# Query norms as the exponentials' scale, and per-head scaling on ScalarE, in a two-layer hybrid encoder trunk

## The chip, the cores and the metric

The kernel runs on one core of one Trainium2 chip. A core has TensorE (PE in the profile, with its weight loads shown as PEld), VectorE (DVE), ScalarE (ACT), GpSimd (POOL) and SyncE (SP), which here only issues DMAs. The time is the device time of one execution in microseconds. Before the change the median of three runs is 590.78 us (590.67 to 590.83).

## The reference

Two layers (`L = 2`) over 256 tokens of width 1024. Each layer normalizes `x`, makes one wide projection, feeds three token mixers (A: gated linear attention, B: sparse attention with an indexer that keeps 64 keys, C: differential attention), gates them, and adds the merged result to `x`:

```
h = _rms(x, norm_g[l]);  proj = h @ w_in[l]           # split into gq gk gv ga gz bq bk bv iq ik iw bz cq ck cv cz gate
_dsa:  q = _rms(bq, qn_g)   # 4 heads of 128;  k = _rms(bk, kn_g)
       p = softmax(q . k over the kept keys);  out = p @ bv
_diff: q = _rms(cq, qn_g)   # 4 heads x 2 halves of 64;  k = _rms(ck, kn_g)
       p = softmax(q_c . k_c) for c in (0, 1);  out = _rms((p0 - lam * p1) @ cv) * (1 - lambda_init)
x = x + (gated sum of y_a @ w_br0, y_b @ w_br1, y_c @ w_br2) @ w_out[l]
```

The part that the change concerns is `_rms` of the queries and keys: each row of each head is divided by its root mean square, which is one number per token and head, called the inverse norm `r` below. A row's softmax takes the maximum of its logits off before the exponential, and divides by the sum after it.

## The kernel before

**Matmuls.** All large products are in float32 precision built of three passes: an operand is held as a rounded high part and a low remainder, and `mm3` (L119) issues high by high, high by low and low by high. The weights stream in as *units* of 128 x 1024 float32. For each unit SyncE issues a DMA into `raw`, ScalarE copies it into `whi` (L234), VectorE subtracts to get `wlo` (L240), and TensorE does, for most projections, 12 matmuls of 128 x 512 with it. Five pairs of `whi`/`wlo` exist, so ScalarE can only begin a unit when TensorE has let go of the pair used five units earlier. Some units are sums of two weight matrices, made by GpSimd's accumulating DMAs (L208). Transposes go through TensorE too (L122).

**Order.** A table `ORDER` says which projection follows which (`bq, cq, ck, gate4, cz, bk, cv, gq, iq, ...`). The mixers are generators ("tasks") that are advanced between matmul groups by `Flow.pump`, and which yield a number of groups to wait. On top of this the framework schedules the program by its own timeline of the engines, so that the final order of the instructions on each engine can differ from the order in which they are written, and moves when an operation goes to another engine.

**Norms.** `headnorm` squares the whole 128 x 512 projection on ScalarE (L396, out of PSUM, the matmul's accumulators), sums the squares by head on VectorE (L398), has GpSimd make `r` (`rstd`: a multiply-add at L294, a power of -1/2 at L295), and multiplies the projection by `r` on VectorE into `qn` (L401). `qn` is transposed on TensorE (L122), and its high and low part are made by ScalarE (L414, L561) and VectorE. This is done for `bq`, `bk` (4 heads of 128) and for `cq`, `ck` (8 halves of 64), two token blocks each. Tiles of the tag `ev` (`sq`, `qn`, `th`) share two buffers; projections share four PSUM tiles (`pj`), logits and transposes four others (`at`).

**Softmaxes.** In `dsa_attend` the logits `blog` are masked on VectorE, the negated row maximum `negm` is taken on VectorE (L721), ScalarE makes the exponential with `negm` as its bias and the row sum as a second output (L688), VectorE multiplies the probabilities by the inverse sum (L730), and TensorE transposes them. In `diff_task` it is the same with L791 and L688; there the two softmaxes are joined on VectorE (L804) and transposed as `pT` (L122), which the products `av` take. Per layer there are three such logit tiles in the sparse attention and six in the differential one.

## Time and profile before

| | us |
|---|---|
| median of three runs | 590.78 (590.67 to 590.83) |
| profiled execution, first to last instruction | 589.0 |
| TensorE busy | 581.9 (99%) |
| VectorE busy | 494.4 (84%) |
| ScalarE busy | 382.9 (65%) |
| GpSimd busy | 89.7 (15%) |

The span of the profiled execution is the time between its first and last instruction; the page gives no other time of that execution. The 1.8 us between this span and the median lie outside the instructions. The granted TensorE clock is 1.000 over the whole span. A row of a group reads: line, engine, operation, output<-inputs, shape, count | busy us, mean ns of one | idle us just before and what ended it. A row of a timeline begins with its start and its length in us.

### The profile page before, as it was taken

What the parts mean: (1) busy time and instruction counts of PE and PEld (TensorE: products, weight loads), DVE (VectorE), ACT (ScalarE), POOL (GpSimd) and SP (SyncE); (2) the same over time, 40 slices, a digit from 0 to 9 for tenths busy, and PEclk for the clock granted to TensorE, in tenths of its full rate; (3) what the DMA queues carried; (4) which work ended last, traced back from release to release, by engine and by line L of the source; (5) the groups of instructions that cost most, each with busy time, mean ns of one, the idle gap of its engine ahead of it and who ended that gap; (6) DMA issues with size and microseconds to landing.
All of it is one profiled execution on the core that took longest, in us unless ns stands there. A gap on an engine that the chain in (4) does not pass through costs nothing.

```text
span 589.0 us, 8836 instructions
## 1 busy us (share of the span) xinstructions
PE 581.9 (99%) x3116; PEld 495.2 (84%) x3116; DVE 494.4 (84%) x815; ACT 382.9 (65%) x655; POOL 89.7 (15%) x121
## 2 busy tenths in 40 slices
PE   8999999999999999999999999999999999999997
PEld 4888888998888988888878888889888889888886
DVE  6878969988999899898687796797989998889962
ACT  6759668786658478464466775776866576656530
POOL 2032212002213031000020340300211221200000
PEclk9999999999999999999999999999999999999999
DMA  8654669428999679565446446862599994974821
GB/s 334 235 197 144 209 235 270 142 104 227 289 293 220 228 225 284 175 221 197 143 145 207 151 149 208 263 205 105 184 260 279 297 242 149 284 236 132 258 75 71
DMA packets 34027, 121.82 MB, mean 207 GB/s; under 512 B 3776, under 2 KB 4160, under 8 KB 33984
## 3 DMA queue, kind: packets, MB, share of 16 engines
q1 hardware_dynamic: 29376, 104.49, 50.5%
q0 software_dynamic: 4608, 16.78, 15.9%
q8 instruction: 24, 0.39, 0.3%
q14 instruction: 19, 0.16, 0.1%
HBM read 120.21 MB, written 1.05 MB: 206 GB/s over the span
## 4 chain that ended last, share of the span: by engine, by line
PE 96%; DVE 1%; DMA 1%; ACT 1%; issue 0%; POOL 0%; SPq 0%; DVEq 0%; POOLq 0%
PE q L119 13%; PE p L119 11%; PE gate L119 7%; PE out L119 7%; PE bz L119 4%; PE iq L119 4%; PE gq L119 4%; PE ck L119 4%; PE cq L119 4%; PE gz L119 4%; PE cz L119 4%; PE gv L119 4%; PE bv L119 4%; PE bk L119 4%; PE cv L119 4%; PE bq L119 3%
## 5 line engine op out<-in xcount | busy, mean ns | idle before, releaser
L234 ACT ACTIVATE whi<-raw 128x1024 fp32r<-128x1024 f32 x172 | 180.9, 1062 | 102.2 <-PE p L119 21.0
L240 DVE TENSOR_TENSOR wlo<-raw,whi 128x1024 fp32r<-128x1024 f32 x172 | 207.9, 1219 | 38.9 <-ACT whi L234 37.6
L234 ACT ACTIVATE whi<-sum 128x1024 fp32r<-128x1024 f32 x32 | 34.1, 1065 | 24.1 <-PE gz L119 5.4
L240 DVE TENSOR_TENSOR wlo<-sum,whi 128x1024 fp32r<-128x1024 f32 x32 | 39.5, 1235 | 4.2 <-ACT whi L234 3.7
L208 POOL DMA_DIRECT2D sum<-in_units x32 | 28.3, 883 | 84.0 <-DMA sum<-in_units 28.2
L294 POOL TENSOR_SCALAR v<-ss 128x4 f32<-128x4 f32 (+1 forms) x24 | 6.9, 288 | 224.0 <-DVE ss L398 91.5
L295 POOL TENSOR_TENSOR r<-v,half 128x4 f32<-128x4 f32 (+1 forms) x24 | 35.5, 1477 | 2.0
L119 PE MATMUL out<-wlo,mTh 128*128 128x512 f32 (+1 forms) x72 | 26.2, 368 | 0.0
L119 PE MATMUL out<-whi,mTh 128*128 128x512 f32 (+1 forms) x72 | 26.0, 366 | 0.0
L119 PE MATMUL out<-whi,mTl 128*128 128x512 f32 (+1 forms) x72 | 25.7, 368 | 0.0
L119 PE MATMUL q<-whi,sl 128*128 128x512 f32 x64 | 25.2, 394 | 0.0
L119 PE MATMUL q<-wlo,sh 128*128 128x512 f32 x64 | 25.1, 392 | 0.0
L119 PE MATMUL q<-whi,sh 128*128 128x512 f32 x64 | 24.9, 390 | 0.0
L119 PE MATMUL gate<-wlo,hTh 128*128 128x512 f32 x64 | 24.9, 390 | 0.0
L119 PE MATMUL p<-wlo,yTh 128*128 128x512 f32 x64 | 24.9, 389 | 0.0
L119 PE MATMUL gate<-whi,hTl 128*128 128x512 f32 x64 | 24.8, 390 | 0.0
L119 PE MATMUL p<-whi,yTl 128*128 128x512 f32 x64 | 24.6, 389 | 0.0
L119 PE MATMUL gate<-whi,hTh 128*128 128x512 f32 x64 | 24.5, 393 | 0.0
L119 PE MATMUL p<-whi,yTh 128*128 128x512 f32 x64 | 24.1, 392 | 0.0
L119 PE MATMUL q<-whi,hTh 128*128 128x512 f32 x48 | 19.2, 400 | 0.0
L119 PE MATMUL q<-whi,hTl 128*128 128x512 f32 x48 | 18.8, 391 | 0.0
L119 PE MATMUL q<-wlo,hTh 128*128 128x512 f32 x48 | 18.8, 391 | 0.0
(352 smaller groups left out, 1748.8 us busy)
## 6 DMA issues: line engine op xcount, KB each, us to landing
raw<-in_units SPq DMA_DIRECT2D x176, 512.0 KB, 4.5
sum<-in_units POOLq DMA_DIRECT2D x32, 512.0 KB, 7.9
sum<-in_units SPq DMA_DIRECT2D x16, 512.0 KB, 6.1
wsr<-in_wsmall SPq DMA_DIRECT2D x2, 416.0 KB, 7.0
xe<-in_x SPq DMA_DIRECT2D x1, 584.0 KB, 3.4
x<-in_x SPq DMA_DIRECT2D x1, 512.0 KB, 7.9
out<-xe SPq DMA_DIRECT2D x2, 256.0 KB, 2.0
pt<-in_ptmp SPq DMA_DIRECT2D x1, 384.0 KB, 9.5
```

The costliest lines, as they stand in the source:

```text
L119: return self.put(nc.tensor.matmul(*a, **k))
L208: G.dma_start(self.sums[l, "t3" if what == "t3" else "t1", pair, i], units[u + i], accum_op=OP.add)
L234: a = A.activation(hi, raw, AF.Copy)
L240: self.splits[j] = (a, V.tensor_sub(lo, raw, hi.bitcast(F32)))
L294: G.tensor_scalar(v, ss, 1.0 / dim, EPS, op0=OP.mult, op1=OP.add)
L295: G.tensor_tensor(r, v, half[:, :n], op=OP.pow)
```

## The change

The projection's squares of `bq` and `bk` (4 heads) are made by four ScalarE instructions per tile, one for each head, with the sum as a second output: VectorE's sum goes. For `cq` and `ck` (8 halves) square and sum stay as they were. The queries `bq` and `cq` are no longer multiplied by `r`: `qn` is a plain copy on ScalarE that needs no `r`. GpSimd copies `r` into a tile `rq`, and the softmaxes use it as the exponential's scale; so the row maximum, taken by VectorE into a tile `max`, has to be multiplied by `r` as well, which a new GpSimd instruction does (`scaled_max`) before the exponential can use it as bias. For the differential attention `rc` is a copy of `rq` in the order of its logits. The sparse keys `bk` are multiplied by `r` on ScalarE, four instructions per tile (`ck` stays on VectorE). The sparse probabilities are multiplied by their inverse sum on ScalarE instead of VectorE, one instruction per head as before. No matmul and no weight DMA is added or removed.

```diff
+    def squares(ps, nh, dh):
+        ss = tiny(nh, "ss")
+        if nh == 4:
+            junk = ev([P, CH], BF16, "sq")
+            for h in range(nh):
+                hs = slice(h * dh, h * dh + dh)
+                A.activation(junk[:, hs], ps[:, hs], AF.Square, accum_out=ss[:, h:h + 1])
+        else:
+            sq = ev([P, CH], F32, "sq")
+            A.activation(sq, ps, AF.Square)
+            V.tensor_reduce(ss, sq.rearrange("p (h d) -> p h d", h=nh), axis=AX, op=OP.add)
+        return rstd(ss, nh, dh)
+
+    def plain(ps):
+        n = ev([P, CH], F32, "qn")
+        A.activation(n, ps, AF.Copy)
+        return n
+
     def headnorm(ps, nh, dh):
-        sq = ev([P, CH], F32, "sq")
-        A.activation(sq, ps, AF.Square)
-        ss = tiny(nh, "ss")
-        V.tensor_reduce(ss, sq.rearrange("p (h d) -> p h d", h=nh), axis=AX, op=OP.add)
-        r = rstd(ss, nh, dh)
+        r = squares(ps, nh, dh)
         n = ev([P, CH], F32, "qn")
-        V.tensor_tensor(n.rearrange("p (h d) -> p h d", h=nh), ps.rearrange("p (h d) -> p h d", h=nh),
-                        r.unsqueeze(2).to_broadcast([P, nh, dh]), op=OP.mult)
+        if nh == 4:
+            for h in range(nh):
+                hs = slice(h * dh, h * dh + dh)
+                A.activation(n[:, hs], ps[:, hs], AF.Copy, scale=r[:, h:h + 1])
+        else:
+            V.tensor_tensor(...)
         return n
...
+        rq = {}
+
+        def row_scale(mark, nh, ps):
+            r = rq[mark] = sp.tile([P, nh], F32, tag="rq", bufs=8, name=nm("rq"))
+            G.tensor_copy(r, squares(ps, nh, CH // nh))
+            return plain(ps)
+
         def cq_task(mark, ps, dst):
-            n = headnorm(ps, 8, 64)
+            n = row_scale(mark, 8, ps)
...
         def qk_task(mark, ps, nh, dh, gain, hi, lo):
-            n = headnorm(ps, nh, dh)
+            n = row_scale(mark, nh, ps) if mark[:2] == "bq" else headnorm(ps, nh, dh)
...
-        def softmax_rows(ps, j, S, p, negm, sums, i):
-            A.activation(p, ps[:, j], AF.Exp, bias=negm[:, i:i + 1], accum_out=sums[:, i:i + 1])
+        def softmax_rows(ps, j, S, p, negm, sums, i, r):
+            A.activation(p, ps[:, j], AF.Exp, bias=negm[:, i:i + 1], scale=r[:, i:i + 1], accum_out=sums[:, i:i + 1])
+
+        def scaled_max(negm, r, ps, i):
+            m = tiny(ps.shape[1], "max")
+            V.tensor_reduce(m, ps, axis=AX, op=OP.max, negate=True)
+            G.tensor_tensor(negm[:, i], m, r[:, i], op=OP.mult)
...
-                V.tensor_reduce(negm[:, h0:h0 + per], ps, axis=AX, op=OP.max, negate=True)
+                scaled_max(negm, rq[f"bq{t}"], ps, slice(h0, h0 + per))
...
-                V.tensor_scalar_mul(p, p, rs[:, h:h + 1])
+                A.activation(p, p, AF.Copy, scale=rs[:, h:h + 1])
...
+            rc = sp.tile([P, 8], F32, tag="rc", bufs=2, name=nm("rc"))
+            G.tensor_copy(rc.rearrange("p (c h) -> p c h", c=2), rq[f"cq{t}"].rearrange("p (h c) -> p c h", c=2))
...
-                    V.tensor_reduce(negm[:, i0:i0 + per], ps, axis=AX, op=OP.max, negate=True)
+                    scaled_max(negm, rc, ps, slice(i0, i0 + per))
```

The framework's schedule puts the instructions in another order. Three places matter below. In the rows a name's number is that of its tile; the second program counts its tiles otherwise, so numbers differ between the two.

ScalarE at the start of the second layer, before the change: after the last square of `x` comes the square of `bq` for the first tokens, and then the eight evacuations of `h`, transposed, of the second tokens (`hps` into `hTh`), for which TensorE waits there.

```order
L320 ACTIVATE junk_3353,ss_77<-x 128x512
L396 ACTIVATE sq_3568<-bq_3417 128x512
L341 ACTIVATE hTh<-hps_3359,xe 128x128
L341 ACTIVATE hTh<-hps_3360,xe 128x128
L341 ACTIVATE hTh<-hps_3367,xe 128x128
```

The same place after the change:

```order
L320 ACTIVATE junk_3397,ss_77<-x 128x512
L400 ACTIVATE sq_3614,ss_3613<-bq_3461 128x128 x4
L409 ACTIVATE qn_3624<-bq_3461 128x512
L341 ACTIVATE hTh<-hps_3403,xe 128x128
L341 ACTIVATE hTh<-hps_3404,xe 128x128
```

Four squares and the copy of `bq` now stand where one square stood, ahead of the evacuations.

TensorE in the projection `iq` of the first layer, where the differential attention's probabilities of the first tokens (`cp`) are transposed into `pT`, before the change (`whi_786` is the third of the four weight units of `iq`):

```order
L119 MATMUL iq_1381<-hTh,whi_786 128x256
L119 MATMUL iq_1381<-hTl,whi_786 128x256
L119 MATMUL iq_1381<-hTh,wlo_787 128x256
L122 MATMUL pT_1366<-xe,cp_1219 128x128 x4
L119 MATMUL iq_1381<-hTh,whi_786 128x256
```

And after it (`whi_759` is the second unit, `whi_798` the third; this is the second of the four passes that `iq` makes over its units, where the rows above are of the first):

```order
L119 MATMUL iq_1419<-hTh,whi_759 128x256
L122 MATMUL pT_1404<-xe,cp_1245 128x128
L119 MATMUL iq_1419<-hTl,whi_759 128x256
L119 MATMUL iq_1419<-hTh,wlo_760 128x256
L122 MATMUL pT_1404<-xe,cp_1245 128x128
L119 MATMUL iq_1419<-hTh,whi_798 128x256
L122 MATMUL pT_1404<-xe,cp_1245 128x128
```

The transposes come 22 instructions later in the program, at 542 instead of 520, and one by one among matmuls of the projection.

TensorE in the projection `gv` of the first layer, before the change (the first and the second half of the tokens are `gv_1692` and `gv_1693`; `whi_905`, `whi_951` and `whi_979` are the second, third and fourth unit):

```order
L119 MATMUL gv_1692<-whi_905,hTl 128x512
L119 MATMUL gv_1692<-whi_951,hTh 128x512
L119 MATMUL gv_1693<-whi_887,hTh 128x512
...
L119 MATMUL gv_1693<-whi_951,hTl 128x512
L119 MATMUL gv_1692<-whi_979,hTh 128x512
L119 MATMUL gv_1692<-wlo_980,hTh 128x512
```

And after it (`whi_917`, `whi_963` and `whi_991` are the second to the fourth unit):

```order
L119 MATMUL gv_1730<-whi_917,hTl 128x512
L119 MATMUL gv_1730<-whi_963,hTh 128x512
...
L119 MATMUL gv_1730<-whi_963,hTl 128x512
L119 MATMUL gv_1730<-whi_991,hTh 128x512
L119 MATMUL gv_1730<-wlo_992,hTh 128x512
```

The first tokens now take all four units one after the other before the second tokens begin, so the fourth unit is used after 18 matmuls of `gv` and not after 36.

More of the change, by code (lines that the diff above doesn't have):

```diff
@@ L392, in proj_first @@
         yield p1
-    def headnorm(ps, nh, dh):
-        sq = ev([P, CH], F32, "sq")
-        A.activation(sq, ps, AF.Square)
-        ss = tiny(nh, "ss")
-        V.tensor_reduce(ss, sq.rearrange("p (h d) -> p h d", h=nh), axis=AX, op=OP.add)
-        r = rstd(ss, nh, dh)
-        n = ev([P, CH], F32, "qn")
-        V.tensor_tensor(n.rearrange("p (h d) -> p h d", h=nh), ps.rearrange("p (h d) -> p h d", h=nh),
-                        r.unsqueeze(2).to_broadcast([P, nh, dh]), op=OP.mult)
+    def squares(ps, nh, dh):
[14 more added lines that the diff above has]
+        return n
+    def headnorm(ps, nh, dh):
+        r = squares(ps, nh, dh)
+        n = ev([P, CH], F32, "qn")
+        if nh == 4:
[3 more added lines that the diff above has]
+        else:
+            V.tensor_tensor(n.rearrange("p (h d) -> p h d", h=nh), ps.rearrange("p (h d) -> p h d", h=nh),
+                            r.unsqueeze(2).to_broadcast([P, nh, dh]), op=OP.mult)
         return n
@@ L720, in dsa_attend @@
                                        op0=OP.mult, op1=OP.add)
-                V.tensor_reduce(negm[:, h0:h0 + per], ps, axis=AX, op=OP.max, negate=True)
+                scaled_max(negm, rq[f"bq{t}"], ps, slice(h0, h0 + per))
                 prob[h0] = w2([P, per, S], F32, "bp")
                 for j in range(per):
-                    softmax_rows(ps, j, S, prob[h0][:, j], negm, sums, h0 + j)
+                    softmax_rows(ps, j, S, prob[h0][:, j], negm, sums, h0 + j, rq[f"bq{t}"])
                 yield 1
@@ L790, in diff_task @@
                     V.memset(ps[0:64, :, S - 64:], NEG)
-                    V.tensor_reduce(negm[:, i0:i0 + per], ps, axis=AX, op=OP.max, negate=True)
+                    scaled_max(negm, rc, ps, slice(i0, i0 + per))
                     p = w2([P, per, S], F32, "cp")
                     for j in range(per):
-                        softmax_rows(ps, j, S, p[:, j], negm, sums, i0 + j)
+                        softmax_rows(ps, j, S, p[:, j], negm, sums, i0 + j, rc)
                     prob[h0, c] = p
```

## The prediction

> **What bounds the kernel now.** I read the head of the page first, then the stretches of the span in the table of windows (columns: stretch, its length, busy us and instructions of PE, PEld, DVE, ACT, POOL, then granted clock, DMA share, GB/s), then the groups.
>
> ```profile
> span 589.0 us, 8836 instructions
> PE 581.9 (99%) x3116; PEld 495.2 (84%) x3116; DVE 494.4 (84%) x815; ACT 382.9 (65%) x655; POOL 89.7 (15%) x121
> PE 96%; DVE 1%; DMA 1%; ACT 1%; issue 0%; POOL 0%; SPq 0%; DVEq 0%; POOLq 0%
> ```
>
> ```profile
> 14.30:296.30 282.00, 281.98 (x1513) 241.87 (x1513) 244.29 (x402) 187.31 (x317) 43.69 (x58) 1.00 0.69 212
> 296.30:299.00 2.70, 2.03 (x12) 1.14 (x11) 1.73 (x4) 2.65 (x8) 0.02 (x1) 1.00 0.74 223
> 299.00:587.00 288.00, 286.54 (x1556) 246.61 (x1554) 239.49 (x388) 183.06 (x309) 42.03 (x53) 1.00 0.64 197
> ```
>
> TensorE is busy without a hole in both layers, and the chain of waits is 96% TensorE. Being busy isn't yet being at its pace, so I looked at the pace in the chain:
>
> ```profile
> 209.01 10.91 PE gate L119 x48
> 198.46 6.99 PE bz L119 x58
> ```
>
> 48 matmuls of 512 columns take 10.91 us, 227 ns each, and 58 of (nearly all) 256 columns 6.99 us, 120 ns each; stretches of the same shapes go at the same pace whatever runs beside them. TensorE sets the time, the others follow. At the layer boundary 2.70 − 2.03 = 0.67 us are open; the first 14.3 us end before any instruction that the change touches. So an engine that gets faster has almost nothing to give, and the change can lose time wherever it makes TensorE wait. The cover against that is the stock of weights:
>
> ```profile
> L234 ACT ACTIVATE whi<-raw 128x1024 fp32r<-128x1024 f32 x172 | 180.9, 1062 | 102.2 <-PE p L119 21.0
> L240 DVE TENSOR_TENSOR wlo<-raw,whi 128x1024 fp32r<-128x1024 f32 x172 | 207.9, 1219 | 38.9 <-ACT whi L234 37.6
> ```
>
> ScalarE idled 102.2 us ahead of its weight copies, mostly because TensorE had not yet released a buffer, and VectorE 38.9 us behind ScalarE. With all pairs full, four units of 12 x 0.227 = 2.72 us lie ahead of TensorE: 10.9 us.
>
> **What is removed from VectorE.**
>
> ```profile
> L398 DVE TENSOR_REDUCE ss<-sq 128x4 f32<-128x512 f32 x8 | 5.4, 678 | 0.7 <-ACT sq L396 0.7
> L401 DVE TENSOR_TENSOR qn<-cq,r 128x512 f32<-128x512 f32 x4 | 2.8, 690 | 5.1 <-POOL r L295 5.1
> L401 DVE TENSOR_TENSOR qn<-bq,r 128x512 f32<-128x512 f32 x4 | 2.8, 690 | 1.2 <-POOL r L295 1.2
> L401 DVE TENSOR_TENSOR qn<-bk,r 128x512 f32<-128x512 f32 x4 | 2.7, 682 | 0.6 <-POOL r L295 0.6
> L730 DVE TENSOR_SCALAR bp<-bp,rs 128x256 f32<-128x256 f32 x8 | 3.0, 440 | 0.0
> L730 DVE TENSOR_SCALAR bp<-bp,rs 128x128 f32<-128x128 f32 x8 | 1.7, 272 | 0.0
> ```
>
> These six rows go entirely: 5.4 + 2.8 + 2.8 + 2.7 + 3.0 + 1.7 = 18.4 us, and VectorE falls from 494 to 476 us. None of it was on TensorE's path, so it is worth 0.
>
> **What is added to ScalarE.**
>
> ```profile
> L396 ACT ACTIVATE sq<-bq 128x512 f32<-128x512 f32 x4 | 2.4, 591 | 1.8 <-PE bq L119 1.8
> L916 ACT ACTIVATE junk<-go 128x128 f32<-128x128 f32 x16 | 4.2, 282 | 0.0
> L916 ACT ACTIVATION_READ_ACCUMULATOR junk<-go 128x1 f32 x16 | 3.4, 215 | 0.0
> 199.32 0.26 ACT L916 ACTIVATE junk<-go 128x128 f32<-128x128 f32 x1
> 200.23 0.22 ACT L916 ACTIVATION_READ_ACCUMULATOR junk<-go 128x1 f32 x1
> ```
>
> The linear attention already squares four heads singly. From the first of such a set to the end of the last read, 200.23 + 0.22 − 199.32 = 1.13 us; one square of 512 costs 0.59. Eight tiles (`bq`, `bk`, two blocks, two layers): 8 x 0.54 = 4.3 us. Eight plain copies at 0.59 (the square's row, the same size out of the same memory) are 4.7. Sixteen scaled copies of `bk` at 0.27 (eight like ones in 2.18 us in the fence after the next) are 4.3. The sixteen probability copies aren't in the trace: at least 0.27 each, 4.3; at most 0.28 for the narrow and, by twice that, 0.56 for the wide, 6.7; I take 5.5, in the middle, since width sets the cost only in part. Together 18.8 us, ScalarE 383 to 402 (68%). It lies in idle time that waits for TensorE except where a TensorE need is near, which the trace shows in three places.
>
> *Start of the second layer.* (Start and length; the square, the transposes, the evacuations, and the first matmul that reads them.)
>
> ```profile
> 304.62 0.60 ACT L396 ACTIVATE sq<-bq 128x512 f32<-128x512 f32 x1 [1.75 <-PE bq L119]
> 305.56 1.03 PE L122 MATMUL hps<-xe,h 128*128 128x128 f32 x8
> 306.08 2.18 ACT L341 ACTIVATE hTh<-hps,xe 128x128 fp32r<-128x128 f32 x8 [0.86 <-PE hps L122]
> 306.50 0.50 PE L119 MATMUL bq<-whi,hTh 128*128 128x512 f32 x1
> ```
>
> Ahead of the evacuations there now stand 1.13 + 0.59 us: the end is 304.62 + 1.72 = 306.34, against the 306.08 at which they began. With the overlap that ends of neighbouring instructions show (four reads and squares sum to 1.99 and took 1.13) it may be 306.1. Bounds 0 and 0.26 us; I take 0.1.
>
> **GpSimd's new hop.** The bias of every exponential now goes VectorE, GpSimd, ScalarE. The trace has no such product of two small tiles; the nearest rows are the norm's two steps:
>
> ```profile
> L294 POOL TENSOR_SCALAR v<-ss 128x4 f32<-128x4 f32 x16 | 3.1, 195 | 189.1 <-ACT junk L815 73.3 <-DVE ss L398 56.6 <-ACT junk L916 38.0
> L295 POOL TENSOR_TENSOR r<-v,half 128x4 f32<-128x4 f32 x16 | 19.0, 1186 | 1.3
> 85.17 0.69 DVE L398 TENSOR_REDUCE ss<-sq 128x4 f32<-128x512 f32 x1 [0.30 <-ACT sq L396]
> 86.02 0.20 POOL L294 TENSOR_SCALAR v<-ss 128x4 f32<-128x4 f32 x1 [22.46 <-DVE ss L398]
> 37.35 2.02 POOL L295 TENSOR_TENSOR r<-v,half 128x4 f32<-128x4 f32 x1
> 327.07 2.59 POOL L295 TENSOR_TENSOR r<-v,half 128x8 f32<-128x8 f32 x1
> ```
>
> VectorE's end to GpSimd's start is 86.02 − 85.86 = 0.16 us. A multiply-add takes 0.20, a power of two tensors 1.19 in the mean, 2.02 in a bad case and 2.59 on twice the width. So a hop costs 0.4 to 2.8 us; a multiplication is nearer to the first, and I take 0.4. There are 9 per layer. Behind a waiting exponential stand, on ScalarE, weight copies and further exponentials; whoever waits for these is TensorE. The 12 copies of `r` are off this path, far ahead of their use. In the sparse attention the products are queued behind GpSimd's accumulating DMAs, which can wait long (us in all, times, longest), but the transposes there follow long after:
>
> ```profile
> POOL sum L208 <- DMA sum<-in_units: 28.2, 9, 7.5
> L688 ACT ACTIVATE bp<-blog,negm x8: 357/422/525, 181.4 to 211.9; 128x128 f32<-128x128 f32 x4, 128x256 f32<-128x256 f32 x4
> L122 PE MATMUL pT<-xe,bp x12: 270/272/287, 193.8 to 222.3; 128*128 128x128 f32 x12
> ```
>
> From the first exponential to the first transpose are 12.4 us, from the last to the last 10.4: a wait of 7.5 is covered. In the new order the matmuls between the first logits and the first transposes grow by 9.2 us, and those between the last logits and the last transposes shrink by 0.2 (columns at 227 ns per 512).
>
> In a sentence apart: the Trainium skill, "SBUF — State Buffer", section "Who interferes with whom", says that a VectorE operation with two SBUF inputs and a GpSimd operation that reads SBUF exclude each other for a whole instruction. Every `wlo` is such an operation of 1.22 us, by which the hop would be up to 0.4 + 1.2 = 1.6 us; the sum below would not move, but a bad hop becomes likelier than by the multiply-add's row alone. The powers of 1.0 and 2.0 us in this trace agree with it.
>
> *The probabilities in `iq`.* (VectorE's joined probabilities, TensorE's transposes of them.)
>
> ```profile
> 109.97 1.11 DVE L804 SCALAR_TENSOR_TENSOR cp<-cp,ratio,cp 128x128 f32<-128x128 f32 x4
> 113.31 0.60 PE L122 MATMUL pT<-xe,cp 128*128 128x128 f32 x4
> ```
>
> They were ready at 111.08 and used at 113.31: 2.2 us of margin. In the new order 2.4 us more matmuls (5,376 more columns, at 227 ns per 512) stand before the transposes, so two hops have 4.6 us, 2.3 each. At 0.4 nothing shows. The fourth weight of `iq` gains too: two groups of exponentials stand ahead of its copy, not three.
>
> *The weights of `gv`.* (The fourth unit's low part; a matmul of that unit, the one on the high part; then the load of all engines in this stretch, and in it VectorE's low parts, L240, alone.)
>
> ```profile
> 132.27 1.23 DVE L240 TENSOR_TENSOR wlo<-raw,whi 128x1024 fp32r<-128x1024 f32 x1
> 140.03 0.39 PE L119 MATMUL gv<-whi,hTh 128*128 128x512 f32 x1
> 126.00:150.00 24.00, 24.00 (x137) 20.73 (x136) 22.38 (x35) 19.05 (x33) 4.74 (x5) 1.00 0.80 250
> 126.00:150.00 24.00, 12.14 (x11) 1.00 0.80 250
> ```
>
> The fourth low part was done at 133.50; its first reader, the next matmul behind the one at 140.03, came 227 ns later, at 140.26: 6.8 us. Needed after 18 matmuls instead of 36, it is wanted 4.1 us earlier; 2.7 us remain. Worth 0.
>
> **Sum**: 0 (VectorE) + 0.1 (second layer's start) + 0 (hops, `iq`, `gv`) = +0.1 us on a profiled span of 589.0. The median stands 1.8 us above that span, outside the instructions, which stays: 590.78 + 0.1 = **590.9 us**. Its own range is 590.3 (most of the boundary's open 0.67 gained) to 591.6 (the 0.26, and half a microsecond of one narrow place).
>
> **Rivals.** *Slow hop (0.15).* If GpSimd needs over 2.3 us per hop, TensorE stands at the probability transposes. For it: the power's 2.02 us, queue waits, 2.59 on eight numbers, and a VectorE 93% busy (22.38 of 24.00) soon after. Against: the multiply-add's 0.20. At 2.8 us, two hops per place lose (2.8 − 2.3) x 2 = 1.0; two places (both token blocks) and two layers: 4 us, 594.8.
>
> *Late `gv` weights (0.09).* VectorE made 11 low parts in those 24 us, 2.0 us per unit with its other work; four units at 0.227 x 6 = 1.36 each are now consumed faster. Beyond (2.0 − 1.36) x 4 = 2.6, the margin of 2.7 is used up. At 2.3 us per unit TensorE loses 3.8 − 2.7 = 1.1 per layer: 593.0. Against: VectorE has less to do.
>
> *VectorE's relief pays (0.06).* If part of TensorE's busy time hides waiting that VectorE ends, up to the boundary's and similar small gaps could close: 0.67 there and as much in 299 to 587 (288.00 − 286.54 = 1.46): 2.1 at most, about 589.0. Against: VectorE waits for ScalarE, not TensorE for VectorE. Beside it the Trainium skill, "Perfetto Trace Analysis", section "Identifying the Most-Contended Engine", judges TensorE by LDWEIGHTS busy share and not by matmul busy share. By that, TensorE's 84% would equal VectorE's 84%, VectorE might bound as well, and removing 18.4 us would give 572.4; the constant 227 ns contradict it, and I give it 0.02 of these 0.06.
>
> **How the numbers follow.** A measurement of this kernel tells a difference from about 0.2%, 1.2 us. Forecast 0.70, of which 0.02 is lost on the slow side by several small stalls; slow hop 0.15, late weights 0.09, relief 0.06. So faster 0.06, same 0.68, slower 0.02 + 0.15 + 0.09 = 0.26. The range reaches to the late weights and part of the slow hop above, and half of the relief below: 589.9 to 593.5.
>
> **What will show it.** Right: TensorE busy in both long stretches to within 0.5 us, 227 ns pace; VectorE near 476 us, ScalarE near 402; the `max` to exponential hop near 0.4 us; evacuations of the second layer beginning within 0.3 us of where the pattern above puts them. Wrong: a TensorE wait at `pT` released by `cp`, at `gv` or `bv` by `wlo`, or at `hTh` by more than 0.3 us; GpSimd products of 1 us and more; or a shorter pitch of the matmuls, which would mean that VectorE or ScalarE had slowed them.

## The result and the profile after

The changed kernel takes 594.83 us (median of four runs, 594.70 to 594.94), beside 590.77 of the kernel before on the same chip: ratio 1.0069, with an interval of 1.0056 to 1.0082. It is 4.1 us slower. The forecast was 590.9 in a range of 589.9 to 593.5, so it was wrong. The profiled execution's span grew by the same 4.1 us. Times are medians of the executions that agree; a single execution, of e3 below, took 1179.96 us and is left out. The head of the page after, and the table of windows with the same stretches as before (columns as there):

```profile
span 593.1 us, 8912 instructions
PE 583.9 (98%) x3116; PEld 495.4 (84%) x3116; DVE 481.2 (81%) x779; ACT 403.1 (68%) x751; POOL 103.8 (18%) x151
PE 88%; DVE 4%; ACT 3%; DMA 2%; issue 1%; POOL 0%; SPq 0%; ACTq 0%; DVEq 0%
```

```profile
14.30:296.30 282.00, 280.89 (x1503) 240.23 (x1504) 235.24 (x382) 196.58 (x365) 51.20 (x72) 1.00 0.69 212
299.00:587.00 288.00, 286.51 (x1543) 245.48 (x1544) 233.04 (x371) 195.21 (x363) 47.30 (x68) 1.00 0.65 197
```

The load moved as the change says: VectorE 494.4 to 481.2 us, ScalarE 382.9 to 403.1. What is new stands in the first stretch: TensorE has 1.1 us without work, where it had 0.02, and the chain of waits falls from 96% to 88% TensorE. The waits of TensorE of 0.5 us and more, before (releaser; us in all, times, longest):

```profile
PE idle L119 <- DVE idle L463: 1.2, 1, 1.2
PE bq L119 <- DVE wlo L492: 1.0, 2, 0.9
PE hps L122 <- DVE h L332: 0.6, 1, 0.6
PE hps L122 <- ACT h L332: 0.5, 1, 0.5
```

After the change these four are there with the same times, and two more:

```profile
PE p L119 <- ACT gate L1149: 1.1, 2, 0.6
PE go L119 <- ACT Sh L301: 0.8, 2, 0.4
```

The two new ones come once per layer each: `go`, the linear attention's product with its state, waits for ScalarE's copy `Sh` of that state; and `p`, the first matmul of the branches' output projections, waits for the hyperbolic tangent of the gate (L1149), which frees the accumulators that `p` writes into. Neither place is among those that the prediction costed. Both traces have the same number of matmul columns, so I compared the times at which equal shares of the columns were done. In the first layer the changed kernel is late by 0.45 us at 50% of the layer (behind `iq` and `gv`), by 1.03 at 70% (behind `go`) and by 2.16 at 80% (behind `p`); from there on nothing is added, the second layer adds the same again, and that makes the 4.1 us.

**`go`.** The last sparse maximum before it, the exponentials and the state's copy; after, in the timeline of VectorE, GpSimd, ScalarE and TensorE (start, length):

```profile
190.43 0.67 DVE L718 TENSOR_REDUCE max<-blog 128x4 f32<-128x512 f32 x1
191.02 1.21 DVE L240 TENSOR_TENSOR wlo<-raw,whi 128x1024 fp32r<-128x1024 f32 x1
191.19 1.10 POOL L719 TENSOR_TENSOR negm<-max,rq 128x4 f32<-128x4 f32 x1 [4.52 <-DVE max L718]
192.99 1.06 ACT L234 ACTIVATE whi<-raw 128x1024 fp32r<-128x1024 f32 x1 [2.11 <-DMA raw<-in_units]
193.96 0.44 ACT L714 ACTIVATE bp<-blog,negm,rq 128x128 f32<-128x128 f32 x1
197.05 0.60 ACT L301 ACTIVATE Sh<-state 128x512 fp32r<-128x512 f32 x1
197.70 0.33 PE L119 MATMUL go<-Sh,q2Th 128*128 128x128 f32 x1 [0.40 <-ACT Sh L301]
```

The same work before:

```profile
179.85 0.67 DVE L721 TENSOR_REDUCE negm<-blog 128x4 f32<-128x512 f32 x1
181.39 0.36 ACT L688 ACTIVATE bp<-blog,negm 128x128 f32<-128x128 f32 x1
184.13 0.60 ACT L301 ACTIVATE Sh<-state 128x512 fp32r<-128x512 f32 x1
188.73 0.22 PE L119 MATMUL go<-Sh,q2Th 128*128 128x128 f32 x1
```

Before, `Sh` was ready at 184.73, 4.0 us ahead of `go`. After, it is ready at 197.65 and `go` starts at once, 0.40 us late by the trace's count. ScalarE's queue now holds, in this order, a weight copy that stood 2.11 us for its DMA, the four exponentials, two copies of the state, and `Sh`.

**`p`.** ScalarE ahead of the gate's tangent, after:

```profile
219.23 0.56 ACT L714 ACTIVATE bp<-blog,negm,rq 128x256 f32<-128x256 f32 x1 [2.20 <-POOL negm L719]
222.26 1.69 ACT L761 ACTIVATE bp<-bp,rs 128x256 f32<-128x256 f32 x4
229.22 0.59 ACT L301 ACTIVATE yTh<-yT 128x512 fp32r<-128x512 f32 x1
229.70 1.05 ACT L234 ACTIVATE whi<-raw 128x1024 fp32r<-128x1024 f32 x1
230.65 1.07 ACT L1149 ACTIVATE gate<-gate 128x512 f32<-128x512 f32 x2
231.28 0.50 PE L119 MATMUL p<-whi,yTh 128*128 128x512 f32 x1 [0.57 <-ACT gate L1149]
```

Before:

```profile
219.95 1.06 ACT L234 ACTIVATE whi<-sum 128x1024 fp32r<-128x1024 f32 x1 [1.66 <-PE gate L119]
223.57 1.08 ACT L1116 ACTIVATE gate<-gate 128x512 f32<-128x512 f32 x2
229.28 0.61 PE L119 MATMUL p<-whi,yTh 128*128 128x512 f32 x2
```

Before, two tangents ran from 223.57, one behind the other; the first, for which `p` waits, was done at 224.17, 5.1 us ahead of `p`. After, ScalarE goes from 219.23 to 231 without a pause: exponentials, weight copies, the four scaled probability copies (1.69 us, new on this engine), more weight copies, and then the tangents at 230.65.

**`iq` and `gv`.** Here no wait is listed. The scheduler now puts the transposes singly and in pairs between the matmuls of `iq`, in eight places where there were four. TensorE after (a matmul of 256 columns follows its predecessor of the same kind after 0.12 us):

```profile
119.92 0.28 PE L119 MATMUL iq<-hTh,whi 128*128 128x256 f32 x1
120.04 0.38 PE L122 MATMUL pT<-xe,cp 128*128 128x128 f32 x2
120.18 0.36 PE L119 MATMUL iq<-hTl,whi 128*128 128x256 f32 x1
120.38 0.28 PE L119 MATMUL iq<-hTh,wlo 128*128 128x256 f32 x1
```

and before, around a group of four:

```profile
113.19 0.28 PE L119 MATMUL iq<-hTh,wlo 128*128 128x256 f32 x1
113.31 0.60 PE L122 MATMUL pT<-xe,cp 128*128 128x128 f32 x4
113.67 0.36 PE L119 MATMUL iq<-hTh,whi 128*128 128x256 f32 x1
113.87 0.28 PE L119 MATMUL iq<-hTl,whi 128*128 128x256 f32 x1
```

Behind the transposes one matmul takes 0.20 us until the next, 0.08 more than the regular 0.12, which looks like a price of each change of kind. It isn't one. From the matmul ahead of the transposes to the second one behind them are 0.46 us with two transposes and 0.68 with four; less two regular pitches that is 0.22 and 0.44, 0.11 us for each transpose in both cases; a single one, at 115.89, makes 0.35 us of it, 0.11 as well. The loss of this stretch lies mostly behind it. I compared points of the program at which both kernels have issued the same matmuls: from the start of `iq` to a point late in `gv` the changed kernel loses 0.11 us in the first layer and 0.09 in the second, and from there to the next such point, behind `gv`, another 0.27 in each. A gap of 0.21 us in it opens between `gv` and the transposes of `yc`.

**The new operations themselves** (tiles, groups and a row of the timeline after; the tile rows give ns as shortest, median, longest):

```profile
L719 POOL TENSOR_TENSOR negm<-max,rc x12: 195/738/1342, 104.3 to 409.0; 128x2 f32<-128x2 f32 x8, 128x4 f32<-128x4 f32 x4
L719 POOL TENSOR_TENSOR negm<-max,rq x6: 194/1057/1556, 191.2 to 508.8; 128x2 f32<-128x2 f32 x4, 128x4 f32<-128x4 f32 x2
L714 ACT ACTIVATE bp<-blog,negm,rq x16: 441/503/565, 194.0 to 510.4; 128x128 f32<-128x128 f32 x8, 128x256 f32<-128x256 f32 x8
L761 ACT ACTIVATE bp<-bp,rs 128x256 f32<-128x256 f32 x8 | 3.4, 494 | 0.0
L761 ACT ACTIVATE bp<-bp,rs 128x128 f32<-128x128 f32 x8 | 2.5, 392 | 0.0
208.32 0.19 POOL L719 TENSOR_TENSOR negm<-max,rq 128x2 f32<-128x2 f32 x1 [2.78 <-DVE max L718]
```

A product on GpSimd takes 0.19 to 1.56 us. Six of the 18 take 0.19 or 0.20 us, like the one at 208.32; no `wlo` or other operation on two tiles was running on VectorE when they began. The ten of 1.0 us and more all ran beside an operation of VectorE, eight of them beside a `wlo`, and ended 0.05 or 0.06 us behind its end: in the rows for `go` above, the `wlo` ends at 191.02 + 1.21 = 192.23 and the product at 191.19 + 1.10 = 192.29. An exponential takes 441 to 565 ns, against 357 to 525 in the row of before that the prediction quotes. A scaled probability copy takes 387 to 496 ns; the sixteen make 7.1 us by their own lengths, but since neighbours overlap, ScalarE is busy with them for 3.4 + 2.5 = 5.9 us.

### The profile page after: what moved, and what is told of

It is laid out like the page before. It is cut to its first block, busy times and chain, and to the rows that moved or that the text cites. A ratio compares the mean times of both kernels' runs of the same rounds, so it can differ in the third digit from the quotient of the medians.

```text
span 593.1 us, 8912 instructions
## 1 busy us (share of the span) xinstructions
PE 583.9 (98%) x3116; PEld 495.4 (84%) x3116; DVE 481.2 (81%) x779; ACT 403.1 (68%) x751; POOL 103.8 (18%) x151
## 4 chain that ended last, share of the span: by engine, by line
PE 88%; DVE 4%; ACT 3%; DMA 2%; issue 1%; POOL 0%; SPq 0%; ACTq 0%; DVEq 0%
PE p L119 11%; PE q L119 9%; PE gate L119 7%; PE out L119 7%; PE iq L119 4%; PE gq L119 4%; PE gv L119 4%; PE ck L119 4%; PE cq L119 4%; PE cz L119 4%; PE bv L119 4%; PE bk L119 4%; PE cv L119 4%; PE bq L119 3%; PE gz L119 3%; PE bz L119 2%
## 5 line engine op out<-in xcount | busy, mean ns | idle before, releaser
L234 ACT ACTIVATE whi<-raw 128x1024 fp32r<-128x1024 f32 x172 | 180.6, 1060 | 92.7 <-PE p L119 18.8
L294 POOL TENSOR_SCALAR v<-ss 128x4 f32<-128x4 f32 (+1 forms) x24 | 9.0, 376 | 170.2 <-ACT sq L400 72.1
L295 POOL TENSOR_TENSOR r<-v,half 128x4 f32<-128x4 f32 (+1 forms) x24 | 30.7, 1278 | 2.0
L714 ACT ACTIVATE cp<-clog,negm,rc 128x128 f32<-128x128 f32 (+1 forms) x32 | 16.0, 515 | 8.9 <-POOL negm L719 8.9
L119 PE MATMUL iq<-hTh,whi 128*128 128x256 f32 x64 | 18.8, 295 | 0.0
```

The source lines that it names most:

```text
L119: return self.put(nc.tensor.matmul(*a, **k))
L234: a = A.activation(hi, raw, AF.Copy)
L294: G.tensor_scalar(v, ss, 1.0 / dim, EPS, op0=OP.mult, op1=OP.add)
L295: G.tensor_tensor(r, v, half[:, :n], op=OP.pow)
L714: A.activation(p, ps[:, j], AF.Exp, bias=negm[:, i:i + 1], scale=r[:, i:i + 1], accum_out=sums[:, i:i + 1])
```

## The experiments

Questions: is it ScalarE's load, GpSimd's hop, the longer exponential, or the order in which the schedule put the queues? Where an edit says "order held", every instruction of TensorE, VectorE, ScalarE and GpSimd is put in the stated order by ordering dependences without a wait; otherwise the schedule is free to change. Ratios are to the kernel before on the same chip, with the 95% interval.

**e1 and e2: each kernel's instructions with the other's order of TensorE.** (Only TensorE's order is held.)

```diff
 # e1: after.py;  e2: before.py
+for a, b in zip(row, row[1:]):        # row: TensorE's instructions as the other kernel has them
+    tc.add_manual_dep(b.ins, a.ins.name, NOSYNC, reason="order")
```

> The changed kernel's instructions, with TensorE's whole order pinned to that of the kernel before; the other engines are ordered by the framework around it. Order theory (the loss of 4.1 us comes from where the new schedule puts the work): back to 590.8 to 591.4, no TensorE wait over 0.3 us at go and p, no lone transposes in iq. Cost theory (the added ScalarE time of about 20 us and the GpSimd hop cost the time wherever they stand): 594 to 596, with waits of TensorE at pT, go or p.

Measured: 595.63 us, 1.0086 (1.0071 to 1.0101). `go` and `p` wait no more, and a new wait takes their place:

```profile
PE clog L167 <- ACT cp L762: 3.1, 4, 0.8
```

In the differential attention, a logit product waits for exponentials to give back its accumulators; two gaps of 0.86 and 1.00 us beyond the regular pitch per layer. Two GpSimd products there took 2.71 us together, ahead of these exponentials.

> The reverse: the kernel before, instruction for instruction, with TensorE's order pinned to that of the changed kernel. Order theory: as slow as the changed kernel or nearly, 593 to 595, with the lone transposes in iq (0.4 us per layer) and the late go. Cost theory: 590.8 to 591.7, only the 0.4 us per layer of the lone transposes remain.

Measured: 597.78 us, 1.0106 (1.0087 to 1.0125).

```profile
PE qkT L173 <- DVE qn L452: 2.5, 2, 1.9
PE p L170 <- ACT gate L1167: 1.0, 2, 0.6
```

The new order of TensorE makes even the old instructions wait at `p`, by the same 0.6 us; and it comes too early for VectorE's normalization of the differential keys. The old order makes the new instructions wait at `clog`. Each of the two orders of TensorE is cut for its own instructions: the order of TensorE alone doesn't explain the loss, and the old one can't simply be kept.

**e3: the product on VectorE instead of GpSimd.**

```diff
-            G.tensor_tensor(negm[:, i], m, r[:, i], op=OP.mult)
+            V.tensor_tensor(negm[:, i], m, r[:, i], op=OP.mult)
```

> The changed kernel, but the row maximum is multiplied by r on VectorE instead of GpSimd, so that there is no hop over GpSimd and its queue. If the hop in the sparse attention (4.0 us from the maximum's end to the product's end at 219.2 us, behind an accumulating DMA, a memset and another DMA) is what makes ScalarE late for the gate's tanh and TensorE wait at p: that wait of 0.6 and 0.5 us and what is around it go, about 2.2 us over both layers, 592.6. If ScalarE's load alone does it: unchanged within 0.5 us, 594.4 to 595.3.

Measured: 596.22 us, 1.0091 (1.0074 to 1.0108), above both expectations. No wait at `go` or `p`; instead `gv` waits 1.7 us in each layer, once for VectorE's `kf` and once for a square on ScalarE. Again another order, and another place that waits. Taking the hop away did not bring the time back.

**e4: the sparse attention's softmax as before; e5: no query scale at all, all else of the change kept; e6: the kernel before with the query scale alone.**

```diff
 # e4 (from after; e5 the same for cq and its logits)
-            n = row_scale(mark, nh, ps) if mark[:2] == "bq" else headnorm(ps, nh, dh)
+            n = headnorm(ps, nh, dh)
-                scaled_max(negm, rq[f"bq{t}"], ps, slice(h0, h0 + per))
+                V.tensor_reduce(negm[:, h0:h0 + per], ps, axis=AX, op=OP.max, negate=True)
 # e6 (from before): row_scale, plain, scaled_max and the exponentials' scale, nothing else
```

> The changed kernel, with the sparse queries bq multiplied by r as the keys are (four ScalarE copies per tile) and the sparse softmax without scale and without the GpSimd product; the differential attention keeps the new form. If the sparse hop makes both late places (go and p): 591.2 to 592.0, the lone transposes of iq remain (0.4 us per layer). If it is ScalarE's load: 594 to 595, as 2.3 us of exponential time is traded for about the same in copies.

> The changed kernel without the queries' part: bq and cq are multiplied by r before the transposes (bq by four ScalarE copies per tile, cq on VectorE as before) and the exponentials have neither scale nor GpSimd product. Kept are the four single squares, the keys' and probabilities' scaling on ScalarE. If the GpSimd hop and what it holds up are the loss: 590.5 to 591.3, the same as the kernel before. If ScalarE's added load is the loss: still 593 or more, as some 13 of the 20 us remain.

> The kernel before with the queries' part alone: bq and cq copied plain, r as the exponentials' scale, the maximum times r on GpSimd. Squares in one piece with VectorE's sums, keys and probabilities scaled on VectorE, as before. If the hop is the loss: 593.5 to 596. If it takes ScalarE's added load as well: 590.8 to 592.

Measured: e4 592.03 us, 1.0020 (1.0011 to 1.0029); e5 591.67, 1.0015 (1.0007 to 1.0024); e6 593.73, 1.0055 (1.0041 to 1.0068). The busy times of e4:

```profile
PE 582.9 (99%) x3116; PEld 495.3 (84%) x3116; DVE 480.1 (81%) x779; ACT 405.1 (69%) x763; POOL 99.0 (17%) x141
```

e4 has **more** work on ScalarE than the change (405.1 against 403.1 us) and loses 1.2 us, not 4.1: the load that went to ScalarE is not the cause. What remains in e4 and e5, 0.4 us per layer, lies in the stretch from `iq` to behind `gv`, as after the change, with no wait that was not there before. e6 shows `p` waiting for the tangent once (1.2 us) and a transpose of normalized keys waiting for VectorE (0.9 us). Without the query scale 0.9 us is lost, with it alone 2.9; the sum, 3.8, is near the 4.1. It is also worth seeing that e4's first sparse maximum comes at 190.38, as late as after the change, without any loss: that lateness alone is harmless.

**e7: order held as after, but the last sparse product ahead of what was queued before it on GpSimd.**

```diff
 # GpSimd's order
+negm<-max,rq
 DMA sum;  memset ck;  DMA sum
-negm<-max,rq
```

> The changed kernel with the order of TensorE, VectorE, ScalarE and GpSimd pinned to what it is, but for one instruction per layer: the last sparse product on GpSimd stands ahead of the two accumulating DMAs (and, in the first layer, the memset) that it stood behind. If the queue makes the hop long, ScalarE late, and TensorE wait at p: the hop falls from 4.0 us to about 1.5, the waits at p (0.57 and 0.5 by the view, 0.73 per layer in the gap) go, 593.4; up to 592.6 if all of the 1.1 us per layer around p goes. If TensorE's wait at p is ScalarE's load whatever the hop: 594.8.

Measured: 594.81 us, 1.0065 (1.0053 to 1.0078): nothing gained. The rows of e7 (with all instructions going through one helper, the lines are that helper's from here on):

```profile
215.31 0.19 POOL L263 TENSOR_TENSOR negm<-max,rq 128x2 f32<-128x2 f32 x1 [1.59 <-DVE max L263]
216.92 0.56 ACT L263 ACTIVATE bp<-blog,negm,rq 128x256 f32<-128x256 f32 x1
221.29 1.06 ACT L263 ACTIVATE whi<-sum 128x1024 fp32r<-128x1024 f32 x1 [1.66 <-PE gate L286]
230.64 0.58 ACT L263 ACTIVATE gate<-gate 128x512 f32<-128x512 f32 x1
```

The hop from the maximum's end to the product's end fell from 4.0 us to 0.3, the exponentials came 2.3 us earlier, and ScalarE then idled until TensorE freed a weight buffer at 221.29. From there its queue runs as before, and the tangent is at 230.64 again. My expectation fell: the length of this hop is not what makes `p` wait.

**e8 to e11: single places of the order mended, all else held as after.**

```diff
 # e8: e7's edit;  iq's transposes in groups;  ScalarE: state copies ahead of 3 of 4 exponentials
 # e9, ScalarE, per layer
+gate<-gate (tanh) x2
 whi<-raw
-gate<-gate (tanh) x2
 # e10, ScalarE, per layer
+bp<-blog x4
 whi<-raw (the one that waits for its DMA)
-bp<-blog x4
 # e11: e9, e10, and iq's transposes in groups
```

> The same with three places mended, all other orders pinned: the product first in GpSimd's queue, the twelve lone or paired transposes of iq brought together in fours, and on ScalarE the three copies of the state (carry, carry, Sh) moved ahead of three of the four exponentials they stood behind (in both layers). If the loss is the sum of the three places, 0.45 (iq) + 0.7 (go) + 1.1 (p) per layer: 590.8 to 591.6. If there are other losses by load: 593 or more.

Measured: 594.91 us, 1.0072 (1.0059 to 1.0084). The transposes in groups gave back next to nothing: from the start of `iq` to behind `gv` e8 is faster than the changed kernel by 0.02 us in the first layer and 0.03 in the second. The wait of `go` only moved, to a sparse logit product that waited 0.5 us for the delayed exponentials; `p` still waited 0.6 twice.

> The changed kernel, all orders pinned; on ScalarE the two tanh of gate0, which free the accumulators that p needs, stand ahead of one weight copy (0.95 us) that they stood behind. If the wait at p (0.73 us per layer, 1.1 with what is around it) is a matter of ScalarE's order in front of it: it goes, 592.6 to 593.4. If the lateness only moves on to the next reader: 594.8.

Measured: 593.30 us, 1.0042 (1.0029 to 1.0054). The wait of `p` is gone and 1.5 us with it, by a swap of two neighbours. ScalarE in e9:

```profile
229.92 1.07 ACT L263 ACTIVATE gate<-gate 128x512 f32<-128x512 f32 x2
230.87 1.06 ACT L263 ACTIVATE whi<-raw 128x1024 fp32r<-128x1024 f32 x1
```

> The changed kernel, all orders pinned; on ScalarE the first four sparse exponentials of each layer stand ahead of the weight copy that waits for its DMA until 193.0 us in the first layer (their bias is there at 192.3). If the late go (0.56 to 0.75 us per layer) is that queueing: it goes, 593.3 to 593.9. If it is the late maximum itself: unchanged, 594.8.

Measured: 594.39 us, 1.0060 (1.0047 to 1.0073). The exponentials start at 192.35 instead of 193.96, `Sh` is done at 196.99 instead of 197.65, and the wait of `go` is gone; 0.4 us by the medians, less than the intervals resolve, and 0.26 and 0.29 us in the two layers by the common points of the traces.

> Both of the last two edits, and the transposes of iq brought together in fours. If the loss is three places of order (0.25 to 0.45 in iq, 0.6 at go, 0.9 at p, per layer): 590.9 to 591.8. If ScalarE's load keeps making something late: 593 or more.

Measured: 592.63 us, 1.0031 (1.0019 to 1.0043). No wait of TensorE is listed that the kernel before didn't have. Of the 4.1 us, 2.2 came back by edits of order alone, with every instruction of the change in place, and the time lies between the two expectations. By the common points of the traces the two layers together gained 1.7 us at `p`, 0.55 at `go` and 0.1 from `iq` to behind `gv`. The rest lies in small gaps, 0.22 us by 60% of the first layer and 0.81 by 80%, of which I placed only 0.2 behind `gv` and 0.3 in `bz`.

**e12: the sparse probabilities scaled on VectorE again, the rest of the order held as after.**

```diff
-                A.activation(p, p, AF.Copy, scale=rs[:, h:h + 1])
+                V.tensor_scalar_mul(p, p, rs[:, h:h + 1])
```

> The changed kernel with the sparse probabilities scaled on VectorE as before (right behind the inverse sum), the orders of everything else pinned: ScalarE loses 7.1 us in sixteen instructions, of which 1.69 us stand ahead of the late tanh in the first layer. If ScalarE's added work is what makes the tanh late: the wait at p goes, 592.6 to 593.4. If the sparse softmax is late for other reasons: 594.3 or more.

Measured: 594.20 us, 1.0060 (1.0048 to 1.0073). The wait of `p` halves:

```profile
PE p L286 <- ACT gate L263: 0.6, 2, 0.3
```

The four copies (1.69 us) stand ahead of the tangent in a queue without slack, so they are part of the delay there. The 0.6 us by the medians are less than the intervals resolve. ScalarE's busy time fell from 403.1 to 398.3 us, 4.8 and not the 7.1 of the expectation, for the reason given above.

**e13 to e18: the order held as after, and only the cost of the query scale taken away.** The queries' inverse norm is left out of the sparse and differential logits here, so the probabilities are others.

```diff
 # e13, e16: product kept, by ones; no scale operand
-A.activation(..., AF.Exp, bias=negm[...], scale=r[...], ...)
+A.activation(..., AF.Exp, bias=negm[...], ...)
 # e14, e17: scale operand kept (ones); the bias is the maximum itself, the product is read by nobody
+A.activation(..., AF.Exp, bias=max[...], scale=ones[...], ...)
 # e15, e18: neither
+A.activation(..., AF.Exp, bias=max[...], ...)
```

In e13 to e15 the ones were a new tile of 128 x 8; in e16 and e17 they lie in an unused part of a tile that is there anyway, and e18 needs none.

> Instructions and every engine's order as after the change, but the exponentials take no scale operand and the product multiplies by a tile of ones (the queries' inverse norm is left out of the sparse and differential logits, so the probabilities are others); the hop over GpSimd stays. If the longer exponentials (0.08 to 0.10 us each, 48 of them) make the state's copy late: the wait of `go` for `Sh` (0.40 us) falls to about 0, since four exponentials ahead of it get 0.4 us shorter; the wait of `p` for the gate's tanh, which the order of ScalarE's queue sets, stays at 0.6; time about 594.0. If the length doesn't matter: 594.8 with both waits as they were. If the queries' scale delays both places by its length alone: 593.0 or less.

> Orders as after the change; the exponentials keep a scale operand (a tile of ones) but take the maximum as bias directly; the product on GpSimd is still made and read by nobody (the inverse norm is left out of the logits, so the probabilities are others). If the hop makes the late places late: 593.0 or less, waits of `go` and `p` gone. If ScalarE's order decides, and the exponentials stand behind a weight copy that waits for its DMA anyway: 594.6 to 594.9, waits as they were.

> Orders as after the change; neither scale operand nor hop (product made, read by nobody; the inverse norm is left out of the logits, so the probabilities are others). What remains above the kernel before is what the new order and the moved work cost alone. If the order decides: 594.0 as without the operand. If the hop and the length of the exponentials are the cause, as the run without the queries' scale suggests: 591.7, its time.

Measured: 599.43 us, 1.0146 (1.0132 to 1.0159); 600.47, 1.0163 (1.0149 to 1.0177); 600.07, 1.0159 (1.0145 to 1.0173). None of the expectations had this. The cause is no wait: the matmuls of the transposed `h` with the weights run at another pace. The same twenty matmuls of the gate in the chain of waits, after the change:

```profile
211.40 4.56 PE gate L119 x20
```

and in e13:

```profile
213.48 4.66 PE gate L286 x20
```

That is 228 and 233 ns for 512 columns. The matmuls of `p` and `out` kept their pace. By the allocation of the two programs, the new tile of 32 bytes per partition moved `whi`, `wlo`, `yTh` and `mTh` by these 32 bytes, and left `hTh` and `hTl`, which lie ahead of it, in place: what slowed down has one operand moved and one not, what kept its pace has both moved. The direction isn't always the same: in `iq` and `bz`, where the weights are loaded and `h` streams through (elsewhere it is the other way round), matmuls of 256 columns came down from 120 to 117 ns.

> As e13 (no scale operand, the product by ones, hop kept, orders as after the change), but the ones lie in an unused part of a tile that is there, so no tile moves. If e13's slower matmuls come from the 32 bytes by which the new tile moved the tiles behind it, the 512-column matmuls are back at 227 ns and the time is 593.9 to 594.3: the wait of `go` gone as in e13, that of `p` still 0.5 to 0.6 per layer. If the missing operand itself slowed them: 599 again.

> As e14 (scale by ones, the maximum itself as bias, the product read by nobody, orders as after the change) at unmoved addresses. If the hop's time isn't what delays `go` and `p`: 594.4 to 594.9, both waits still there (0.4 and 0.5 per layer). If it is: 593 or less.

> As e15 (neither operand nor hop, orders as after the change) at unmoved addresses. If the order costs most: 593.6 to 594.2, `p` still waiting 0.5 to 0.6 per layer. If the queries' scale does by itself: 591.7.

Measured: e16 594.26 us, 1.0062 (1.0047 to 1.0077); e17 595.40, 1.0072 (1.0055 to 1.0089); e18 594.30, 1.0060 (1.0045 to 1.0075). With the weights and `h` at their old addresses the pace is 227 ns again. The waits of TensorE in e18:

```profile
PE p L286 <- ACT gate L263: 1.1, 2, 0.6
PE go L286 <- ACT Sh L263: 1.0, 2, 0.8
```

With neither operand nor hop, in the same order, the kernel is still at 594.3, and `p` waits exactly as long as after the change. The wait of `go` in e18 is longer in the second layer, where the weight ahead of the exponentials kept ScalarE waiting for 3.04 us instead of 2.15; the profiled execution of e18 was the slowest of its four, at 595.25 us. In e16 the wait of `go` falls from 0.8 to 0.2 us, and the traces gain 0.24 and 0.49 us in the stretch around it; a transpose that waits 0.3 us for VectorE's `qn` early in the second layer is new there and takes 0.48 us of it back. In e17 both waits stay (`go` 1.2 us in all, `p` 1.1), and the time is above the expectation of 594.4 to 594.9. So the hop's own time is worth nothing that can be measured in this order (e17), the operand's about half a microsecond by the medians (e16, within the intervals), and the order carries the rest: e5, scheduled anew without the query scale, is at 591.67, and e18 in the order that was made for the query scale at 594.30, 2.6 us apart. Their instructions are not quite the same: e18 still copies the queries plainly and makes the products. But it has no more of the load, with ScalarE busy for 398.9 us against 400.7 in e5 and VectorE for 480.2 against 482.5.

## Why the prediction was wrong

- **TensorE bounds, so relief on VectorE is worth 0**: right in what it was worth. VectorE lost 13.2 us of its busy time, not 18.4: the six rows did go, but others grew, above all two `nf` from 0.28 to 1.18 us. Nothing was gained. The rival with a gain fell, and with it the figure of 572.4 that followed from the weight loads' share.
- **ScalarE's addition, 18.8 us, lies in idle time**: the sum was near (20.2), in part by luck. The exponentials were assumed unchanged; with a scale from a tile 48 of them cost 4.1 us more. Against that the squares and the plain copies held ScalarE's queue for 3.6 and 4.1 us more, not 4.3 and 4.7, and unrelated rows shrank by about 1.5. The probability copies, taken at 5.5 within 4.3 to 6.7, are right with 5.9 us busy. As load the addition did no harm (e4). As places in a queue it did: the copies stand ahead of the tangent (e12). The Trainium skill, "ScalarE: Activation LUTs", section "What ACT_TABLE_LOAD costs", has the rule that I should have looked up: an activation takes 186 ns and 0.833 ns per element, and about 93 ns more for each operand of one number per partition that is read from a tile. By it the lengths of the sixteen copies are estimated at 8 x 386 + 8 x 493 ns = 7.0 us and the 48 exponentials at 48 x 93 ns = 4.5 us more; the traces agree, with 7.1 and 4.1.
- **Start of the second layer, 0.1 (0 to 0.26)**: right. From the first square to the evacuations are 308.18 − 306.69 = 1.49 us, where they were 306.08 − 304.62 = 1.46.
- **GpSimd's hop, 0.4 us, "nearer to the first"**: right for six of the 18 products, 0.19 us like the multiply-add, and wrong for most: in the median they took 0.74 and 1.06 us. The long ones ended with an operation of VectorE beside them. The Trainium skill, "SBUF — State Buffer", section "Who interferes with whom", speaks of exclusion between VectorE's two-input operations and GpSimd, which gave up to 1.6 us for a hop; the products' 0.19 to 1.56 us and their common ends with `wlo` agree with that. The powers, which the prediction named in its favour, do so only in part: after the change a power at 319.57 took 1.01 us with no operation of VectorE beside it. But e17 shows that this error alone cost nothing in the order as it was made.
- **The cover in the sparse attention**: this is the step that failed. I measured the exponentials against their own readers, the transposes 10 to 12 us later, and that cover held: no transpose waits. The prediction said that "weight copies and further exponentials" stand behind a waiting exponential. Behind them also stood `Sh` and the gate's tangents, with TensorE's `go` and `p` as readers, and I did not look up where these two stood in the new order. Before, they had margins of 4.0 and 5.1 us; after, none, and TensorE waited 0.8 and 1.1 us for them over both layers.
- **`iq`, 2.3 us of margin per hop**: right for the wait, which didn't come, and for the single transposes, which I priced at 0: grouping them gave back 0.02 to 0.08 us per layer (e8, e11). The stretch still lost about 0.4 us per layer, most of it behind `gv`, where I priced nothing.
- **`gv`'s weights, 2.7 us of margin**: right. No `wlo` wait appears there.
- **The slow-hop rival** gave 594.8, the measured time, by accident: it placed the loss at the probability transposes and at the differential and sparse blocks' hops. There is no wait there, and with the hop taken away (e17) the loss stays.

In place of the failed step the runs show this. The query scale costs 2 to 3 us, for the most part not by its own operations in their queue, but because the schedule that is made with it puts ScalarE's instructions in an order in which `go` and `p` have no slack. For `p` this is shown from both sides: a swap of order takes its wait away (e9), and taking the scale's operations out of the same order leaves it as it was (e18). For `go` the swap (e10) and the shorter exponentials (e16) each take most of the wait away. All swaps together (e11) give back 2.2 us; taking the scale's operations out gives back 0.5 (e18), within the intervals. Why the schedule chose this order, by its own timeline, no run shows; e3 and e6 suggest only that each set of instructions gets an order with some tight place of its own. Open is also the 1.8 us that e11 keeps. No variant was as fast as the kernel before; the best, e5, was 0.9 us slower.

## What to carry to other kernels

In a kernel whose bound engine has no hole, a moved operation is not priced by its duration or by the margin of its own readers: for each in-order queue that it joins, list what stands behind it until the next idle time and look for the first reader on the bound engine. Where a scheduler makes the order, compare the whole new order of each queue with the old one and look up the margin of every instruction that the bound engine reads, also of those that the change doesn't touch. To separate order from cost, hold the order and take the operations away, and hold the operations and swap two neighbours; and when a test needs a tile, take it from one that is there.

## What the runs showed of the hardware

- An exponential on ScalarE with its scale read from a tile takes 85 to 89 ns longer than without in the same order of instructions: 466 against 381 ns on 128 x 128, 564 against 475 on 128 x 256 (after the change against e16, means of sixteen each). In the kernel before, in another order, the same exponentials took 361 and 486 ns.
- GpSimd's product of two tiles of 128 x 2 or 128 x 4 takes 0.19 us, and up to 1.56 us in the same execution. The ten of 1.0 us and more ended 0.05 or 0.06 us behind a `wlo` or `se` of VectorE that ran beside them.
- A transpose of 128 x 128 between float32 matmuls of 256 columns costs TensorE 0.11 us, alone (0.35 us from the matmul ahead to the second behind, less 2 x 0.12), in a pair (0.46 us, less the same) and in a group of four (0.68 us, less the same).
- Moving the weights' tiles by 32 bytes per partition against the transposed `h` slowed the 512-column matmuls between them from 228 to 233 ns, over 2%, and this kernel by 5 to 6 us (e13 to e15 against e16 to e18). Matmuls whose two operands had both moved kept their pace, and those of 256 columns in `iq` and `bz`, where the weights are loaded and `h` streams through, went from 120 to 117 ns. Whether the distance of the operands or the address of one decides was not tried.
